# Four seven-product blocks per FFN, a third weight sum by transfer, x sums from PSUM, and a written list for splits and sums

## The chip, the cores and the metric

One core of a Trainium2 chip runs the kernel in one launch. The metric is device time in microseconds (us), the median of several executions.

## The reference

A trunk of two layers on `x` of 256 tokens and 1024 features, float32. Each layer is: a feed-forward network (FFN), a mixer (bidirectional mLSTM in layer 0, windowed attention in layer 1), and a second FFN, each with a residual and a layer norm. Cut to what matters:

```python
def swiglu(x, w_in, w_out):                 # w_in 1024 x 5632, w_out 2816 x 1024
    gu = x @ w_in
    g, u = gu[..., :D_FF], gu[..., D_FF:]
    return (jax.nn.silu(g) * u) @ w_out

for l in range(2):
    x = layer_norm(ALPHA * x + 0.5 * swiglu(x, ffn_w_in[l, 0], ffn_w_out[l, 0]), ...)
    y = mlstm_mixer(x, ...) if l == 0 else window_attention(x, ...)
    x = layer_norm(ALPHA * x + y, ...)
    x = layer_norm(ALPHA * x + 0.5 * swiglu(x, ffn_w_in[l, 1], ffn_w_out[l, 1]), ...)
```

So there are six stages: FFN, mLSTM, FFN, FFN, attention, FFN.

## The kernel before

*Precision.* Every operand of a large product is kept as two `fp32r` tiles: a high half (a cast on ACT, `w_hi`) and a low half (value minus high half, a subtraction on DVE, `w_lo`). A product takes three matmuls: high-high, high-low, low-high (`mm3`).

*Weights.* All weights of all stages go through one object, `Weights`. A *word* is 512 KB of weights, loaded into a raw tile by SP's queue (`w_raw`, 4 buffers, and `s_raw`, 6 buffers, for words that are added to each other; two more buffers `v_raw` in the FFNs). A *split* makes a high and a low half of a raw tile; `plan` is the fixed order of all splits, and PE uses them in that order. At most 10 splits are in the ring (`RING`): a new one needs the oldest to be used up. `high()` emits the cast, `low()` the subtraction, `sum()` the sum of two raw tiles; `sum()` is a DVE addition where both tiles are there, and where the second summand is a weight block in HBM it is an accumulating DMA issued from POOL's queue. `low()` frees the raw tile when it has no more uses, and `load()` issues the next loads.

*An FFN.* Eight `wide` words give the first 512 columns of `g` and `u`. Then follow three groups, each a *unit* and a *seven-product block*. A unit is 256 columns of `g` and of `u`, four words (`beside`), 48 matmuls of 512 columns. A seven-product block gives 512 columns of each. It regards the tokens as two halves and the features as two halves and multiplies the 2 x 2 blocks in seven products instead of eight, 84 matmuls: four products use sums of blocks of x (`S1` to `S4`) and sums of weight blocks. With `b11`, `b12` the first feature half of `g` and `u` and `b22` the second half of `u`, `b11` is split four times: as loaded, after adding `b12`, after adding `b22`, and after adding the second half of `g` from HBM (by transfer). `b12` is split once, after a sum with `b22` on DVE. That makes 14 splits, six DVE sums (`s_raw<-s_raw`) and two accumulating transfers a block. The x sums are taken from `xr`, two tiles that DVE adds from the high and low halves of the transposed x.

Behind a chunk of columns, the products with `w_out` follow as *down* rows: `down(n)` takes n splits and adds 12 matmuls each into the four `py` banks of PSUM. Six down rows are left for the end of the FFN, then come the norm and the transposes of the new x (`py` banks, `to_xT`). 22 down rows, 84 splits per FFN in all.

*Order of the work.* Each engine runs its instructions in the order in which the program emits them. Within FFNs a planner (`Paced`, with fixed costs per instruction) keeps an estimated time per engine and decides after each matmul whether a high half, a low half or a sum is emitted there (`fill`). In the other stages hand-written tables (`PU`, `TD`, `MP`, `PD`) say how many splits are emitted at which place.

In the profile almost all instructions carry L134, the line of the recording call of the planner; L263 is the accumulating transfer in `sum()`. Tiles are therefore told apart by name: `pw` and `py` are PSUM banks, `hh`, `e`, `g` the evacuated products, `h_hi`/`h_lo` their transposes.

Of the kernel before, what the change touches and what calls it, by code (L numbers as in the profile page):

```python
# [1 line left out]

# [15 lines left out]
S = 256  # L18
# [3 lines left out]
F = 2816  # L22
UNITS = F // 256
GROUPS = 3
# [4 lines left out]
PU = [3, 1, 2, 1, 1, 1, 1, 1, 0, 1, 1, 2]  # L29
# [4 lines left out]
TD = [0, 3, 2, 0, 2, 2]  # L34
MP = [1, 0, 0, 0, 1, 0, 1, 1, 0, 0, 0, 0, 2, 2, 2]
PD = [8, 0, 5, 9, 6]
# [3 lines left out]
AHEAD = 300.0  # L40
SOON = -1000.0
LANDING = 2200.0
LOADING = 1340.0
SECOND = 1250.0
ADDING = 8000.0


class Paced:

    def __init__(self, nc):
        self.nc = nc
        self.pe = self.vec = self.act = self.dma = 0.0
        self.there, self.places = {}, {}
        self.filler, self.alone = None, True
        self.vector = Engine(nc.vector, self.on_vector)
        self.scalar = Engine(nc.scalar, self.on_scalar)
        self.tensor = Engine(nc.tensor, self.on_tensor)
# [3 lines left out]

    def place(self, ap):

        f = ap.ap[0][0]
        key = (ap.offset % f if f else 0, tuple(ap.ap[1:]))
        if key not in self.places:
            i = np.array([key[0]])
            for step, n in key[1]:  # L70
                i = (i[:, None] + step * np.arange(n if step else 1)[None, :]).reshape(-1)
            self.places[key] = i
        return self.places[key]

    def when(self, *aps):
        t = 0.0
        for ap in aps:
            a = self.there.get(ap.name)
            if a is not None:
                i = self.place(ap)  # L80
                t = max(t, a[i[i < a.size]].max(initial=0.0))
        return t

    def mark(self, ap, t):
        i = self.place(ap)
        a = self.there.get(ap.name)
        if a is None or a.size <= i.max():
            self.there[ap.name] = np.zeros(int(i.max()) + 1)
            if a is not None:
                self.there[ap.name][:a.size] = a  # L90
        self.there[ap.name][i] = t

    def load(self, ap, source, engine=None):
        if engine is not None:
            engine.dma_start(ap, source)
        elif isinstance(source, list):
            for k, src in enumerate(source):
                self.nc.sync.dma_start(ap[:, k].rearrange("p (m f) -> p m f", m=src.shape[1]), src)
        else:
            self.nc.sync.dma_start(ap, source)  # L100
        come = self.pe + LANDING
        alone, self.alone = self.alone, come > self.dma
        self.dma = max(self.dma, come) + LOADING + (SECOND if alone and not self.alone else 0.0)
        self.mark(ap, self.dma)

    def on_vector(self, name, n, out, ins):
        self.vec = max(self.vec, self.when(*ins)) + (n + 71) / 0.96
        for o in out:
            self.mark(o, self.vec + 115)

    def on_scalar(self, name, n, out, ins):
        self.act = max(self.act, self.when(*ins)) + n * 0.912 + 25
        for o in out:
            self.mark(o, self.act + 125)

    def on_tensor(self, name, n, out, ins):
        self.pe = max(self.pe, self.when(*ins)) + (109.0 if name == "transpose" else n / 2.4 + 13.3)
        for o in out:
            self.mark(o, self.pe + 200)
        if self.filler is not None:  # L120
            self.filler()


class Engine:
    def __init__(self, engine, told):
        self.engine, self.told = engine, told

    def __getattr__(self, name):
        f = getattr(self.engine, name)
        if name.startswith("preload"):  # L130
            return f

        def call(out, *args, **kw):
            r = f(out, *args, **kw)  # L134
            ins = [x for x in [*args, *kw.values()] if hasattr(x, "ap")]
            outs = [out] + ([kw["accum_out"]] if "accum_out" in kw else [])
            size = lambda x: int(np.prod(x.shape[1:]))
            self.told(name, size(out) if name in ("matmul", "transpose") else max(map(size, [out] + ins)), outs, ins)
            return r
        return call  # L140


class Weights:
# [5 lines left out]
    def __init__(self, nc, pool, words, plan, after):  # L149
        self.nc, self.pool, self.words, self.plan, self.after = nc, pool, words, plan, after  # L150
        self.raw, self.parts, self.half, self.sums = {}, {}, [], []
# [4 lines left out]
        self.uses = [0] * len(words)  # L156
        for p in plan:
            self.uses[p["word"]] += 1
# [45 lines left out]
    def split(self, upto):  # L204
        while self.made < min(upto, len(self.plan)):
            self.high()
        while self.half and self.half[0][0] < upto:
            self.low()

    def high(self):  # L210

        nc, i = self.nc, self.made
        p = self.plan[i]
        while self.half and (p["word"] not in self.raw or any(h[0] == p["needs"] for h in self.half)):
            self.low()
        while any(s_[0] == p["needs"] or p["word"] not in self.raw for s_ in self.sums):
            self.sum()
        if p["word"] not in self.raw:
            return False
# [12 lines left out]
        return True  # L232

    def low(self):

        nc = self.nc
# [13 lines left out]
        self.sums += [(i, *sum_) for sum_ in self.after.get(i, ())]  # L250
# [3 lines left out]
    def sum(self):  # L254
        nc = self.nc
        _, w, v = self.sums.pop(0)
# [5 lines left out]
        else:  # L262
            nc.gpsimd.dma_start(t.rearrange("p (k f) -> p k f", k=self.words[w]["k"]), v, accum_op=OP.add)  # L263
            nc.mark(t, max(nc.vec, nc.pe) + ADDING)

    def fill(self):

        nc = self.nc
        while True:
            act, vec = max(nc.act, nc.pe), max(nc.vec, nc.pe)  # L270
            if act < nc.pe + AHEAD and len(self.half) < 2 and self.made < min(self.room, len(self.plan)):
                p = self.plan[self.made]
                if (p["word"] in self.raw and nc.when(self.raw[p["word"]]) < act + SOON
                        and not any(p["needs"] == x for x in [h[0] for h in self.half] + [s_[0] for s_ in self.sums])):
                    self.high()
                    continue
            if vec < nc.pe + AHEAD:
                if self.half and nc.when(self.half[0][1]) < vec + SOON:
                    self.low()
                    continue  # L280
                if self.sums and nc.when(*(self.raw[w] for w in self.sums[0][1:] if isinstance(w, int))) < vec + SOON:
                    self.sum()
                    continue
            break

    def take(self, n):
        i = self.used
        self.used += n
        self.split(self.used)
        return [self.parts[j] for j in range(i, i + n)]  # L290
# [4 lines left out]
    def done(self, upto=None, most=None, high_only=False):  # L295

# [5 lines left out]
        if self.nc.filler is not None:  # L302
            self.fill()
            return
        end = min(self.room if most is None else min(self.room, self.made + most), len(self.plan))
        while self.made < end and self.high():
            pass
        if not high_only:
            self.lows()

    def lows(self):
        while self.half:
            self.low()
# [3 lines left out]
def trunk_kernel(ctx: ExitStack, tc: tile.TileContext, x, ffn_w_in, ffn_w_out, ln_g, ln_b, ml_w_in, ml_gate_b,  # L317
                 ml_norm_g, ml_w_out, at_w_in, at_sink, at_w_out, out):
    nc = Paced(tc.nc)
# [40 lines left out]
    def seven(w, c0, c1, downs):  # L360

        at = lambda r0, c: [two(w, r0 + 256 * j, c) for j in range(2)]
        b12, b11, b22 = ([word(x, 2, "s_raw") for x in at(*p)] for p in ((0, c1), (0, c0), (512, c1)))
# [3 lines left out]
        for j in range(2):  # L367
            after[s1[j]] = [(b11[j], b12[j])]
        downs(0)
# [15 lines left out]
    for j, (kind, l, i, _) in enumerate(stages):  # L385
        if kind == "ffn":
# [10 lines left out]
            for g in range(GROUPS):  # L397
                c0 = 512 + 768 * g
                for a in range(4):
                    beside(wi, a * 256, c0, F + c0)  # L400
                down(2)
                seven(wi, c0 + 256, F + c0 + 256, lambda i_: down(1) if g < GROUPS - 1 or i_ < 2 else None)
            down(6)
# [32 lines left out]
    W = Weights(nc, wpool, words, plan, after)  # L436
    load_x(0, 0)
# [61 lines left out]
    def to_xT(t, src, bank, halves=range(2)):  # L499
        for h in halves:  # L500
# [3 lines left out]
            split_evac(pair(xT, A, slice(4 * h, 4 * h + 4), tok(t)), p)  # L504

    def warm(n):

        p = ybank((128, 4, 128))
# [12 lines left out]
    class Norm:  # L521
# [9 lines left out]
        def finish(self, spare):  # L531
# [10 lines left out]
            if len(cuts) == 1:  # L542
                W.done(0, spare)
# [5 lines left out]
            if len(cuts) > 1:  # L549
                W.done(0, spare)  # L550

    def tail(y, h, todo, first, norm, last, turn_at, between=None):

        for t in range(2):
            for o in range(2):
                final = t == 1 and o == 1
                for n, (c, (i, w)) in enumerate(todo[t]):
# [6 lines left out]
                    if final and n >= turn_at - 1:  # L564
                        W.done(i + 1, (0, 3, 0)[min(n - turn_at + 1, 2)])
                norm[t].half(o, y[t][o])
            norm[t].finish(t)
        W.done(most=TD[bound[0]])
# [6 lines left out]
    def ffn(l, i, n, pending, last):  # L575
        with ExitStack() as ph:
# [11 lines left out]
            if start:  # L588
                warm(10)
                to_xT(0, xt[0], ybank, (0,))  # L590
                W.split(1)
# [770 lines left out]
```

## Time and profile before

| what | value |
|---|---|
| time, median of 3 runs (lowest, highest) | 942.11 us (941.06, 942.29) |
| span of the profiled execution | 941.2 us |
| busy: PE, DVE, ACT, POOL | 98%, 85%, 58%, 11% |
| matmuls on PE | 4416 |
| moved by DMA | 187.54 MB, mean 199 GB/s |
| last matmul to the end of the span | 7.5 us |

The profiled execution has no time of its own beside its span; the median of the timed runs stands 0.9 us above the span. Busy shares are averages over the six stages; the FFNs run about from 0 to 188, 306 to 481, 481 to 660 and 761 to 941 us. A line of a group gives the count, busy time and mean duration in ns, then the engine's idle time just ahead and what ended it. Durations overlap a little where an engine is pipelined, so the time from start to start is shorter than the duration.

### The profile page before, as it was taken

The numbers are of one execution on the slowest core, as the hardware profiler recorded it, in microseconds if no ns is written. First come the engines' busy times: TensorE is split into PE (matmuls) and PEld (weight loads), VectorE is DVE, ScalarE is ACT, GpSimd is POOL, SyncE is SP. The second block draws the span as 40 slices with busy tenths as digits, with TensorE's granted clock in tenths as the row PEclk, the third lists the DMA queues.
The fourth block names the chain that finished last, engine by engine and source line by source line (L and its number), as shares of the span: only waits on it lengthen the run. The fifth ranks groups of instructions, "written<-read, shape, count | busy, mean of one in ns | idle before, by whom it ended". The sixth has DMA issues, their size and how long they took to land.

```text
span 941.2 us, 12338 instructions
## 1 busy us (share of the span) xinstructions
PE 925.3 (98%) x4416; PEld 766.4 (81%) x4416; DVE 800.0 (85%) x943; ACT 546.5 (58%) x781; POOL 103.2 (11%) x162
## 2 busy tenths in 40 slices
PE   9999999999999999999999999999999999999996
PEld 7788888889878787888888888887887788888885
DVE  6899997787697889988888899977878888898975
ACT  5656756347563548565535566563678554757460
POOL 0030101011111000101010101010544300000100
PEclk9999999999999999999999999999999999999999
DMA  7969773646534949685549597746543266769531
GB/s 267 358 154 338 209 265 75 216 134 204 177 108 145 314 150 327 173 327 134 180 155 338 132 324 210 249 90 200 175 147 104 68 215 254 229 219 306 162 91 45
DMA packets 98461, 187.54 MB, mean 199 GB/s; under 512 B 6720, under 2 KB 37456, under 8 KB 98400
## 3 DMA queue, kind: packets, MB, share of 16 engines
q1 hardware_dynamic: 91072, 173.04, 53.1%
q0 software_dynamic: 6752, 12.66, 8.4%
q10 hardware_dynamic: 576, 1.05, 0.3%
q8 instruction: 35, 0.57, 0.2%
q14 instruction: 26, 0.21, 0.1%
HBM read 185.68 MB, written 1.05 MB: 198 GB/s over the span
## 4 chain that ended last, share of the span: by engine, by line
PE 73%; DVE 12%; DMA 6%; ACT 4%; issue 3%; POOL 1%; SPq 0%; DVEq 0%; ACTq 0%
PE pw L134 46%; PE py L134 27%; DVE w_lo L134 5%; DMA w_raw<-in_ffn_w_in_dram 3%; ACT w_hi L134 2%; DMA w_raw<-in_ffn_w_out_dram 1%; DVE s_raw L134 1%; DMA s_raw<-in_ffn_w_in_dram 1%; ACT sc L134 1%; DVE h L134 1%; DVE o L134 1%; DVE e L134 1%; DMA w_raw<-in_ml_w_in_dram 0%; DVE pr_lo L134 0%; ACT xT_hi L134 0%
## 5 line engine op out<-in xcount | busy, mean ns | idle before, releaser
L134 DVE TENSOR_TENSOR w_lo<-w_raw,w_hi 128x1024 fp32r<-128x1024 f32 (+1 forms) x237 | 280.9, 1216 | 16.0 <-ACT w_hi L134 14.0
L134 ACT CAST w_hi<-w_raw 128x1024 fp32r<-128x1024 f32 (+1 forms) x237 | 240.4, 1049 | 75.4 <-DMA w_raw<-in_ffn_w_out_dram 21.7
L134 PE MATMUL pw<-w_hi,xT_hi 128*128 128x512 f32 x560 | 222.6, 397 | 0.2 <-ACT xT_hi L134 0.2
L134 PE MATMUL pw<-w_hi,xT_lo 128*128 128x512 f32 x560 | 218.9, 391 | 0.2 <-DVE xT_lo L134 0.2
L134 PE MATMUL pw<-w_lo,xT_hi 128*128 128x512 f32 x560 | 218.3, 390 | 0.2 <-DVE w_lo L134 0.2
L134 ACT CAST w_hi<-s_raw 128x1024 fp32r<-128x1024 f32 x144 | 148.4, 1052 | 94.1 <-DVE s_raw L134 58.3
L134 DVE TENSOR_TENSOR w_lo<-s_raw,w_hi 128x1024 fp32r<-128x1024 f32 x144 | 172.6, 1219 | 19.2 <-ACT w_hi L134 19.1
L134 PE MATMUL py<-w_hi,h_hi 128*128 128x512 f32 x352 | 138.2, 393 | 0.3 <-ACT h_hi L134 0.3
L134 PE MATMUL py<-w_hi,h_lo 128*128 128x512 f32 x352 | 137.4, 390 | 0.2 <-DVE h_lo L134 0.2
L134 PE MATMUL py<-w_lo,h_hi 128*128 128x512 f32 x352 | 137.1, 390 | 0.2 <-DVE w_lo L134 0.2
L134 PEld LDWEIGHTS pw<-w_hi,xT_lo 128*128 128x128 f32 x560 | 105.1, 188 | 23.7 <-DVE xT_lo L134 1.0
L134 PEld LDWEIGHTS pw<-w_lo,xT_hi 128*128 128x128 f32 x560 | 105.4, 188 | 21.3 <-DVE w_lo L134 0.9
L134 PEld LDWEIGHTS pw<-w_hi,xT_hi 128*128 128x128 f32 x560 | 105.3, 188 | 21.0 <-ACT xT_hi L134 1.0
L134 DVE TENSOR_TENSOR s_raw<-s_raw 128x1024 f32<-128x1024 f32 x72 | 87.0, 1219 | 0.6
L263 POOL DMA_DIRECT2D s_raw<-in_ffn_w_in_dram x24 | 29.2, 1215 | 496.9 <-DVE w_lo L134 378.7
L134 PEld LDWEIGHTS py<-w_hi,h_lo 128*128 128x128 f32 x352 | 66.1, 188 | 15.2 <-DVE h_lo L134 1.4
L134 PEld LDWEIGHTS py<-w_lo,h_hi 128*128 128x128 f32 x352 | 66.1, 188 | 13.9 <-DVE w_lo L134 0.6
L134 PEld LDWEIGHTS py<-w_hi,h_hi 128*128 128x128 f32 x352 | 66.1, 188 | 13.9 <-ACT h_hi L134 0.7
L134 PE MATMUL pw<-w_hi,S_hi 128*128 128x512 f32 x192 | 74.7, 389 | 0.0
L134 PE MATMUL pw<-w_hi,S_lo 128*128 128x512 f32 x192 | 74.7, 389 | 0.0
L134 PE MATMUL pw<-w_lo,S_hi 128*128 128x512 f32 x192 | 74.7, 389 | 0.0
L134 DVE TENSOR_TENSOR h_lo<-pw,h_hi 128x512 fp32r<-128x512 f32 x44 | 30.1, 687 | 24.5 <-ACT h_hi L134 24.4
(218 smaller groups left out, 1118.1 us busy)
## 6 DMA issues: line engine op xcount, KB each, us to landing
w_raw<-in_ffn_w_out_dram SPq DMA_DIRECT2D x88, 512.0 KB, 5.3
s_raw<-in_ffn_w_in_dram SPq DMA_DIRECT2D x72, 512.0 KB, 6.1
w_raw<-in_ffn_w_in_dram SPq DMA_DIRECT2D x56, 512.0 KB, 5.2
w_raw<-in_ffn_w_in_dram SPq DMA_DIRECT2D x96, 256.0 KB, 4.7
s_raw<-in_ffn_w_in_dram POOLq DMA_DIRECT2D x24, 512.0 KB, 6.1
w_raw<-in_ml_w_in_dram SPq DMA_DIRECT2D x24, 512.0 KB, 4.6
w_raw<-in_at_w_in_dram SPq DMA_DIRECT2D x12, 512.0 KB, 3.8
w_raw<-in_ml_w_out_dram SPq DMA_DIRECT2D x8, 512.0 KB, 3.8
```

The source lines that it names most:

```text
L134: r = f(out, *args, **kw)
L263: nc.gpsimd.dma_start(t.rearrange("p (k f) -> p k f", k=self.words[w]["k"]), v, accum_op=OP.add)
```

## The change

- The FFN's parts become: first chunk, block, block, unit, block, block, six down rows (`PARTS`). Four seven-product blocks and one unit instead of three of each; down rows follow the first two blocks one after each of four steps, two follow the unit, and the last block has two.
- Within a block `b12` gets its third summand from HBM, the second half of `u`, by an accumulating transfer right after its use as a summand, instead of a DVE sum with `b22` after the third split of `b11`. Four DVE sums and four accumulating transfers a block instead of six and two.
- The x sums no longer go through `xr`. They read the PSUM banks in which the transposes of x lie (`xp`); one bank is copied to SBUF by ACT (`a21`), since an operation reads one of its two inputs there.
- The planner and the tables are gone. A string, `ORDER`, lists all high halves (H), low halves (L), sums on DVE (S) and sums by transfer (A) of the whole kernel, each with the number of engine operations that are emitted since the previous entry. After every operation of any stage, entries that are due are emitted if what they need is there. What PE needs at once is emitted in any case.
- The warm-up transposes use a `pw` bank.

```diff
-GROUPS = 3
+PARTS = [("s", (1, 1, 1, 1)), ("s", (1, 1, 1, 1)), ("u", 2), ("s", (1, 1, 1, 1)), ("s", (1, 1, 0, 0))]
+TAIL = 6
+BY_DMA = (0, 1)
...
+ORDER = (
+    "H19L0H16L0H33L3H2L4H3H7L2H2L1L5H38H9L0L1S6H2L4H2L0S0H3H3H5L3L3H5L1L12S3S0A8A5H8L3A4H2L2A2H0H2L1H2H0H0H0H0L4L12"
...
 class Engine:
...
-            self.told(name, size(out) if name in ("matmul", "transpose") else max(map(size, [out] + ins)), outs, ins)
+            c.n += 1
+            if c.then is not None:
+                c.then()
...
+    def ready(self, what):
+        if what == "L":
+            return bool(self.half)
+        if what in self.sums:
+            q = self.sums[what]
+            return bool(q) and all(w in self.raw for w in q[0][1:] if isinstance(w, int)) and not any(
+                x[0] == q[0][0] for x in (self.sums["S"] if what == "A" else ()))
+        p = self.plan[self.made] if self.made < min(self.room, len(self.plan)) else None
+        return p is not None and p["word"] in self.raw and not any(
+            x[0] == p["needs"] and (len(x) == 2 or x[1] == p["word"])
+            for x in self.half + self.sums["S"] + self.sums["A"])
+
+    def run(self, upto=0):
+
+        while True:
+            early = self.made < upto or self.half and self.half[0][0] < upto
+            next_ = [(o[0], what) for what, o in self.order.items()
+                     if o and (early or o[0][0] <= self.nc.n) and self.ready(what)]
+            if not next_:
+                assert not early, (self.made, self.used, self.nc.n)
+                break
+            _, what = min(next_)
+            self.order[what].pop(0)
+            self.high() if what == "H" else self.low() if what == "L" else self.sum(what)
...
     def seven(w, c0, c1, downs):
 
         at = lambda r0, c: [two(w, r0 + 256 * j, c) for j in range(2)]
-        b12, b11, b22 = ([word(x, 2, "s_raw") for x in at(*p)] for p in ((0, c1), (0, c0), (512, c1)))
+        b11, b12, b22 = ([word(x, 2, "s_raw") for x in at(*p)] for p in ((0, c0), (0, c1), (512, c1)))
         s1 = [split_of(w_) for w_ in b11]
         for a in at(512, c0):
             piece(a, 2)
-        for j in range(2):
+        t3 = [None, None]
+        for j, a in enumerate(at(512, c1)):
             after[s1[j]] = [(b11[j], b12[j])]
+            if j in BY_DMA:
+                after[s1[j]].append((b12[j], a))
+                t3[j] = s1[j]
         downs(0)
         s5 = [split_of(w_, None, p) for w_, p in zip(b11, s1)]
         for j in range(2):
             after[s5[j]] = [(b11[j], b22[j])]
         s6 = [split_of(w_, None, p) for w_, p in zip(b11, s5)]
         for j, a in enumerate(at(512, c0)):
-            after[s6[j]] = [(b11[j], a), (b12[j], b22[j])]
+            after[s6[j]] = [(b11[j], a)]
+            if j not in BY_DMA:
+                after[s6[j]].append((b12[j], b22[j]))
+                t3[j] = s6[j]
         downs(1)
-        [split_of(w_, None, p) for w_, p in zip(b12, s6)]
+        [split_of(w_, None, p) for w_, p in zip(b12, t3)]
         for w_ in b22:
             split_of(w_)
         downs(2)
         [split_of(w_, None, p) for w_, p in zip(b11, s6)]
         downs(3)
...
             split_evac(pair(xT, A, slice(4 * h, 4 * h + 4), tok(t)), p)
+            xp[t, h] = p
...
-            def x_raw(t):
-                nc.vector.tensor_add(xr[t], xT[0][:, :, tok(t)].bitcast(F32), xT[1][:, :, tok(t)].bitcast(F32))
...
+            def x_copy():
+                f1["a21"] = temp("a21").rearrange("p (k m) -> p k m", k=4)
+                nc.scalar.copy(f1["a21"], xp[1, 0])
 
             def x_one():
-                f1["S1"] = x_sum("S1", xr[1][:, low], OP.subtract, xr[1][:, high])
+                f1["S1"] = x_sum("S1", f1["a21"], OP.subtract, xp[1, 1])
 
             def x_two():
-                f1["S2"] = x_sum("S2", f1["S1"], OP.subtract, xr[0][:, low])
+                f1["S2"] = x_sum("S2", f1["S1"], OP.subtract, xp[0, 0])
...
-            for g in range(GROUPS):
+            turns = [lambda t=t: tr(hB0, t, hs[t]) for t in range(0 if start else 1, 2)]
+            for g, (what, n_) in enumerate(PARTS):
+                if what == "u":
+                    turns = [unit(turns)]
+                    down(n_)
+                else:
+                    turns = [seven(n_, turns)]
```

More of the change, by code (lines that the diff above doesn't have):

```diff
@@ L263, in sum @@
             nc.gpsimd.dma_start(t.rearrange("p (k f) -> p k f", k=self.words[w]["k"]), v, accum_op=OP.add)
[L264 to L284, printed above, removed]
     def take(self, n):
@@ L301, in done @@
         self.room = max(self.room, upto + RING)
[L302 to L313, printed above, removed]
+        self.run()
 @with_exitstack
@@ L436, in trunk_kernel @@
     W = Weights(nc, wpool, words, plan, after)
+    W.room = RING
+    nc.then = W.run
     load_x(0, 0)
```

260 lines of the change are left out of this document (91 added, 169 removed).

## The prediction

> **What bounds the kernel now.** I read the page first, for the busy shares, and then the chain of work that ended last.
>
> ```profile
> span 941.2 us, 12338 instructions
> PE 925.3 (98%) x4416; PEld 766.4 (81%) x4416; DVE 800.0 (85%) x943; ACT 546.5 (58%) x781; POOL 103.2 (11%) x162
> PE 73%; DVE 12%; DMA 6%; ACT 4%; issue 3%; POOL 1%; SPq 0%; DVEq 0%; ACTq 0%
> ```
>
> PE is busy 98% of the span, yet only 73% of the chain is PE's. So there are places where PE has just been fed in time and the chain runs through whoever fed it. The chain in order of time shows both kinds. First a stretch in which PE alone sets the pace, then the start of the second feed-forward network (FFN):
>
> ```profile
> 66.65 5.44 PE pw L134 x24
> 80.71 11.37 PE pw L134 x52
> ...
> 320.74 11.74 DMA w_raw<-in_ffn_w_out_dram
> ...
> 351.48 2.27 DVE w_lo L134 x2
> 353.75 2.28 DVE s_raw L134 x2
> ...
> 363.19 2.27 DVE w_lo L134 x2
> ...
> 366.93 3.38 PE pw L134 x16
> ```
>
> 24 matmuls of 512 columns in 5.44 us are 0.2267 us each; the 52 are 48 of those and 4 transposes, so a transpose takes (11.37 - 48 x 0.2267)/4 = 0.12 us. From 313 to 367 us the chain leaves PE and goes through loads and then DVE. The stretches of time show how little room there is:
>
> ```profile
> core 0: us, PE busy (x) PEld busy (x) DVE busy (x) ACT busy (x) POOL busy (x), PEclk, DMA share, GB/s
> 306.00:366.00 60.00, 59.82 (x272) 48.68 (x270) 52.25 (x55) 36.21 (x45) 2.67 (x3) 1.00 0.75 241
> 366.00:481.00 115.00, 114.13 (x522) 94.09 (x521) 101.30 (x106) 66.20 (x80) 6.27 (x5) 1.00 0.66 211
> 660.50:761.00 100.50, 97.57 (x507) 79.25 (x505) 83.51 (x135) 68.54 (x164) 42.20 (x92) 1.00 0.37 119
> 80.71:128.41 47.70, 47.70 (x218) 39.47 (x217) 44.76 (x46) 32.27 (x38) 2.49 (x2) 1.00 0.83 283
> ```
>
> The first two rows are the second FFN: 175.0 us, PE 173.95 busy, DVE 153.6. The third row is the attention stage, where PE shows 2.9 us idle. The last is one whole group of the first FFN (unit, seven-product block, six down rows): PE never idle, DVE busy 44.76 of 47.70. PE bounds the kernel; DVE is right behind it in the FFNs. The granted clock is 1.00 everywhere that matters.
>
> **The change, part by part.** Counts are from the diff and from the order in which the changed kernel's instructions stand on each engine.
>
> *PE.* A seven-product block does with 84 matmuls what two units do with 96. There are four instead of three per FFN, so 12 fewer in each of four FFNs: 48 x 0.2267 = 10.9 us off the engine that is never idle. The number of transposes stays.
>
> *DVE.* The durations as they follow each other:
>
> ```profile
> 337.02 2.35 DVE L134 TENSOR_TENSOR s_raw<-s_raw 128x1024 f32<-128x1024 f32 x2
> 339.29 0.74 DVE L134 TENSOR_TENSOR hh<-sg,pw 128x256 f32<-128x256 f32 x2
> 339.95 1.22 DVE L134 TENSOR_TENSOR w_lo<-s_raw,w_hi 128x1024 fp32r<-128x1024 f32 x1
> ...
> 349.06 0.69 DVE L134 TENSOR_TENSOR h_lo<-pw,h_hi 128x512 fp32r<-128x512 f32 x1 [0.28 <-ACT h_hi L134]
> 349.67 1.22 DVE L134 TENSOR_TENSOR w_lo<-s_raw,w_hi 128x1024 fp32r<-128x1024 f32 x1
> L134 DVE TENSOR_TENSOR xr<-xT_hi,xT_lo x8: 1217/1218/1222, 17.1 to 775.2; 128x1024 f32<-128x1024 f32 x8
> L134 DVE TENSOR_TENSOR S_lo<-S,S_hi 128x512 fp32r<-128x512 f32 x16 | 11.1, 692 | 15.5 <-ACT S_hi L134 15.5
> ```
>
> Two weight sums take from 337.02 to 339.29, 1.135 us each; a 512-column operation 349.67 - 349.06 = 0.61; a 256-column one (339.95 - 339.29)/2 = 0.33. A split's low half and an `xr` addition have the size of a sum, so 1.135 too. Per FFN: 6 splits more (+6.8: four blocks of 14 and a unit of 4 against three of each), 2 weight sums fewer (16 against 18, -2.3), both `xr` additions gone (-2.3), one more block's evacuation (5 + 2 operations of 512, +4.3), two units' fewer (2 x (2 x 0.33 + 0.61), -2.5). Net +4.0 us, 15.9 over four FFNs: 816 of some 930 us, 88%. In the second FFN 157.6 against 175.0 - 2.7 = 172.3 us of PE, 91%. That still fits, but only on average.
>
> *The tight stretch.* Before, a unit with its down rows stood between any two seven-product blocks; now the blocks stand in pairs, and the first comes straight after the first chunk. A block with four down rows holds 84 + 48 = 132 matmuls and 8 transposes: 29.9 + 1.0 = 30.9 us of PE. DVE has 18 splits (20.4), 4 sums (4.5) and 7 operations of 0.61 (4.3): 29.2 us, 94%, for 62 us in a row. The last group row above shows 94% on DVE over 47.7 us with PE never idle, so it can be done, if DVE hardly waits. Where DVE waited before, the list acts: the `S_lo` operations stood idle 15.5 us for `S_hi`, about 3.9 per FFN just ahead of the tight place. In the changed order of the later FFNs a low half of a weight stands between each `S` and its `S_lo`, so I count that wait as gone there; in the first FFN two of the four still follow directly.
>
> *Transfers.* The plain loads keep their bytes (66 words per FFN); 10 accumulating transfers per FFN are added, 40 in all, 21 MB.
>
> ```profile
> q1 hardware_dynamic: 91072, 173.04, 53.1%
> q0 software_dynamic: 6752, 12.66, 8.4%
> 112.00:128.00 16.00, 16.00 (x74) 13.23 (x73) 14.73 (x16) 12.24 (x15) 0.00 (x0) 1.00 1.03 390
> s_raw<-in_ffn_w_in_dram POOLq DMA_DIRECT2D x24, 512.0 KB, 6.1
> L263 POOL DMA_DIRECT2D s_raw<-in_ffn_w_in_dram x24 | 29.2, 1215 | 496.9 <-DVE w_lo L134 378.7 <-DVE e L134 45.4 <-DVE S L134 36.6
> ```
>
> At full load plain words move at 390 GB/s: 0.524 MB in 1.34 us. Queue 0 is nearly only the 24 accumulations: 8.4% of 941.2 us over 24 is 3.3 us of all 16 engines each. A block with four down rows now asks for 12 x 1.34 + 4 x 3.3 = 29.3 us of transfer in 30.9 us, 95%; a whole FFN 66 x 1.34 + 16 x 3.3 = 141 of 172, 82%. That is the second thin margin, and no row of before shows accumulations beside a full load queue. Their issue costs POOL 40 x 1.2 = 49 us on an engine 11% busy: nothing, except in the first FFN, where the accumulations of the second block's `b11` stand behind the small loads on POOL's queue.
>
> *The chain within a block.*
>
> ```profile
> L134 ACT CAST w_hi<-s_raw 128x1024 fp32r<-128x1024 f32 x144 | 148.4, 1052 | 94.1 <-DVE s_raw L134 58.3 <-PE pw L134 15.2 <-issue 13.6
> ```
>
> The last use of `b11` needs: low half of its second difference done, accumulation (6.1 us to landing, the row further up), high half on ACT (1.05), low half. In the changed order seven low halves stand on DVE in between: 7 x 1.135 = 7.9 us of cover against 7.15. Before, two more sums of 1.135 stood there. It holds with 0.8 us if the accumulation finds the engines as free as before.
>
> *ACT* gets 24 more casts of 1.05 and two or three more copies and activations per FFN, about 30 us on 546.5; hidden, at 62% busy. *The x sums* now read the transposes' PSUM banks, so the four `py` banks are held until the last sum; the first down row comes after it in program order and starts late only if DVE is late there. *The list* takes splits out of the norm and attention code. The stalls it could remove outside the FFNs are the 2.9 us of the attention row and little else; I take 2 off.
>
> *The sum.* 941.2 - 10.9 = 930.3. The start of each FFN was already set by DVE and loads (chain rows from 320.74 on). There the unit's PE time (72 matmuls, 16.3 us) no longer covers the first block, while DVE loses only 6 splits, 2 sums, 2 `xr`, the unit's three operations and the 3.9 us wait, 6.8 + 2.3 + 2.3 + 1.3 + 3.9 = 16.6. The two balance to 0.3 us, so each FFN start stays as tight as it was, and any late transfer shows on PE. I bound what is lost there at 0 and 3 us per FFN (the 11.74 us landing in the chain is some 6 us over the accumulation's 6.1, and half of that has no cover) and take 1.2: +5. With -2 for attention the span comes to 933, and the timed runs' median stands 942.1 - 941.2 = 0.9 above the span: **934 us**.
>
> **The rivals.**
>
> *The list feeds PE everywhere.* No new stall and the 2.9 us of attention gone with those at FFN starts: 941.2 - 10.9 - 4 + 0.9 = 927. For it: low halves stand between dependent operations wherever I looked. Against it: DVE at 94% and transfers at 95% at the same time.
>
> *Accumulations land late and the kernel becomes slower.* The place is the last use of `b11`, and that of `b12`, in the back-to-back blocks. Sharing the engines with four plain words (4 x 1.34) moves a landing from 6.1 to 11.4 us, 4.5 past the cover of 7.9 less the cast. Over a pair of blocks DVE then idles 9 us; the run-ahead absorbs about 4 in the first pair and all in the second, so PE loses 5 to 6 per FFN: 930.3 + 22 + 0.9 = 953. It decides from about 2.7 us lost per FFN, which gives the 10.9 back. Against it: in the row from 112 to 128 us the engines were full for 16 us and PE ran through. [...]
>
> *The gain is given back.* DVE waits a little in every block, 2 to 3 us per FFN: 930.3 + 10 + 0.9 = 941, no change. The DVE share of 94% speaks for it, the removed `S_lo` waits against.
>
> **How the numbers follow.** My forecast (929 to 938) gets 0.50, the list that feeds PE everywhere (below 929) 0.22, the gain given back (938 to 946) 0.14, late accumulations (above 946) 0.14. The range of 8 in 10 takes in the forecast, most of the better case and part of the third: 925 to 945. A difference of 0.2%, 1.9 us, is about what a measurement of this kernel can tell from no change (its three runs lie within 1.2 us). Below 940.2 lie the first two and a third of the third case, 0.77; within 0.2% 0.07; slower 0.16.
>
> **What would show it.** Right: `x512` matmul groups with 48 fewer instructions at the same pace; PE still at 98%; DVE near 816 us; the chain's DVE pieces again only at FFN starts. Late accumulations would show as ACT `w_hi` waiting for `s_raw` transfers, landings well above 6.1 us, and PE waiting for DVE `w_lo` in the second block of a pair. Given-back gain would show as a PE share of 96 to 97% without such landings. A time under 927 would say that the FFN starts had slack that I did not see.

## The result, and the profile after

| | before | after |
|---|---|---|
| time, median (lowest to highest) | 941.84 us (941.06 to 942.29) | 935.93 us (935.19 to 937.32) |
| ratio | 1 | 0.9942, 95% interval [0.9929, 0.9955] |
| span of the profiled execution | 941.2 us | 933.4 us |

The change makes the kernel 5.9 us faster. The profiled execution of after took 935.19 us, 1.8 us over its span, and the other executions of the two kernels whose span is known stand 1.7 or 1.8 us above theirs. By that, as an estimate, the profiled execution of before, of span 941.2, took some 942.9 us, a little more than its median: the spans differ by 7.8 us, the medians by 5.9.

First the page of after: span and busy shares, the queue of the accumulating transfers, the chain by engine, and their landing (issues, KB each, median us from issue to landing).

```profile
span 933.4 us, 12378 instructions
PE 914.4 (98%) x4368; PEld 756.3 (81%) x4368; DVE 812.3 (87%) x955; ACT 574.3 (62%) x813; POOL 147.0 (16%) x202
q0 software_dynamic: 17632, 33.64, 21.6%
PE 75%; DVE 12%; DMA 5%; ACT 4%; issue 2%; POOL 0%; SPq 0%; DVEq 0%; ACTq 0%
s_raw<-in_ffn_w_in_dram POOLq DMA_DIRECT2D x64, 512.0 KB, 7.5
```

The 48 matmuls are gone, PE is still at 98% and has 75% of the chain (73% before), and DVE has 12 us more to do. Now both spans are cut into their six stages, each stage beginning with PE's first transpose of its new x: FFN, mLSTM, FFN, FFN, attention, FFN. Columns are as in the prediction's stretches of time (stretch, its length, busy us with count of PE, PEld, DVE, ACT and POOL, granted clock, DMA share, GB/s). Before:

```profile
0.00:185.96 185.96, 183.56 (x830) 151.43 (x831) 158.89 (x167) 109.51 (x132) 15.24 (x22) 1.00 0.74 238
185.96:296.70 110.74, 109.18 (x648) 95.54 (x647) 86.25 (x144) 60.20 (x113) 14.73 (x23) 1.00 0.47 153
296.70:478.79 182.09, 181.04 (x824) 148.62 (x823) 160.39 (x168) 106.75 (x128) 10.22 (x8) 1.00 0.68 220
478.79:658.19 179.40, 179.11 (x817) 147.53 (x816) 158.13 (x166) 104.26 (x126) 10.14 (x8) 1.00 0.68 217
658.19:753.04 94.85, 91.92 (x482) 74.60 (x481) 78.10 (x126) 65.35 (x160) 42.20 (x92) 1.00 0.38 123
753.04:941.20 188.16, 180.54 (x823) 148.65 (x821) 158.23 (x172) 100.42 (x122) 10.62 (x9) 0.99 0.60 190
```

After:

```profile
0.00:186.09 186.09, 181.18 (x819) 148.49 (x819) 161.27 (x169) 117.72 (x142) 26.37 (x32) 1.00 0.90 263
186.09:295.45 109.36, 108.15 (x648) 95.56 (x647) 86.83 (x146) 59.38 (x112) 15.21 (x23) 1.00 0.49 159
295.45:474.44 178.99, 178.03 (x811) 146.37 (x810) 163.01 (x171) 113.89 (x137) 22.41 (x18) 1.00 0.85 250
474.44:653.19 178.75, 177.12 (x805) 145.16 (x804) 160.22 (x169) 111.13 (x134) 22.28 (x18) 1.00 0.84 244
653.19:746.65 93.46, 91.31 (x482) 74.64 (x481) 78.40 (x128) 66.11 (x160) 39.04 (x92) 1.00 0.41 132
746.65:933.40 186.75, 178.55 (x811) 146.05 (x809) 162.54 (x176) 106.03 (x129) 21.74 (x19) 0.99 0.76 221
```

Each FFN should be 12 x 0.2267 = 2.72 us shorter. The second is (182.09 - 178.99 = 3.10). The first is no shorter at all (+0.13), the third and fourth by 0.65 and 1.41. So the four FFNs give back (what each falls short of 2.72) 2.85, -0.38, 2.07 and 1.31, together 5.85 of the 10.9 us. In a second profile of the changed kernel, of span 932.2 us, they give back 3.16, -0.26, 0.55 and 1.06, so one stage in one profile is known to about 1.5 us. The mLSTM and attention stages became 1.38 and 1.39 shorter. In sum -10.9 + 5.85 - 2.77 = -7.8, the difference of the spans.

Where PE still waits in the FFNs is seen at the start of the second. DVE's timeline of after (start, us, instruction, and in brackets idle time ahead and who ended it) runs from the low half of the transposed first chunk, `h_lo`, to `hh`, the next thing that PE needs:

```profile
317.59 0.69 DVE L94 TENSOR_TENSOR h_lo<-pw,h_hi 128x512 fp32r<-128x512 f32 x1 [0.67 <-ACT h_hi L94]
318.20 0.68 DVE L94 TENSOR_TENSOR S<-S,py 128x512 f32<-128x512 f32 x1
318.79 1.22 DVE L222 TENSOR_TENSOR w_lo<-w_raw,w_hi 128x1024 fp32r<-128x1024 f32 x1
319.93 0.68 DVE L94 TENSOR_TENSOR S_lo<-S,S_hi 128x512 fp32r<-128x512 f32 x1
...
323.47 1.21 DVE L222 TENSOR_TENSOR w_lo<-w_raw,w_hi 128x1024 fp32r<-128x1024 f32 x1
324.60 0.68 DVE L94 TENSOR_TENSOR S_lo<-S,S_hi 128x512 fp32r<-128x512 f32 x1
325.20 0.68 DVE L94 TENSOR_TENSOR hh<-sg,pw 128x512 f32<-128x512 f32 x1
```

DVE never idles in these 8.3 us: the x sums, their low halves and, between each sum and its low half, one weight's low half stand ahead of `hh`, and DVE took them one after the other, started 0.59 to 1.14 us apart. PE has 4 transposes and 36 matmuls (these 8.16 us) meanwhile, started before `h_lo` did, and then waits 1 us. PE's list of waits for the whole of after (us in all, times, longest) begins with this kind of wait; the list of before has none for `hh`:

```profile
PE pw L94 <- DVE hh L94: 3.1, 4, 1.0
```

In the stretch behind it, two blocks back to back, PE does not pause:

```profile
326.41:385.50 59.09, 59.09 (x268) 48.41 (x267) 53.45 (x54) 39.30 (x47) 8.46 (x7) 1.00 0.92 259
```

The four waits for `hh` are one at the start of each FFN. The chain (start, us, what) shows one more place, in the last pair of blocks of the third FFN:

```profile
618.52 9.43 DMA s_raw<-in_ffn_w_in_dram
...
633.36 1.14 DVE w_lo L222
```

A transfer that landed after 9.4 us was late for one block, and PE stood idle for 1.05 of the 8 us from 632 to 640. In the second profile of the changed kernel this place has no wait, and its third FFN took 177.2 us instead of 178.75.

### The profile page after: what moved, and what is told of

It is laid out like the page before. It is cut to its first block, busy times and chain, and to the rows that moved or that the text cites. A ratio compares the mean times of both kernels' runs of the same rounds, so it can differ in the third digit from the quotient of the medians.

```text
span 933.4 us, 12378 instructions
## 1 busy us (share of the span) xinstructions
PE 914.4 (98%) x4368; PEld 756.3 (81%) x4368; DVE 812.3 (87%) x955; ACT 574.3 (62%) x813; POOL 147.0 (16%) x202
## 3 DMA queue, kind: packets, MB, share of 16 engines
q0 software_dynamic: 17632, 33.64, 21.6%
q10 hardware_dynamic: 576, 1.05, 0.3%
HBM read 206.65 MB, written 1.05 MB: 223 GB/s over the span
## 4 chain that ended last, share of the span: by engine, by line
PE 75%; DVE 12%; DMA 5%; ACT 4%; issue 2%; POOL 0%; SPq 0%; DVEq 0%; ACTq 0%
PE pw L94 48%; PE py L94 28%; DVE w_lo L222 5%; DMA s_raw<-in_ffn_w_in_dram 2%; ACT w_hi L204 2%; DVE s_raw L236 1%; DMA w_raw<-in_ffn_w_out_dram 1%; DVE e L94 1%; ACT sc L94 1%; DVE S L94 1%; DVE h_lo L94 1%; DVE rm L94 1%; DVE S_lo L94 0%; DVE o L94 0%; DVE h L94 0%
## 5 line engine op out<-in xcount | busy, mean ns | idle before, releaser
L204 ACT CAST w_hi<-s_raw 128x1024 fp32r<-128x1024 f32 x192 | 197.4, 1051 | 112.6 <-DVE s_raw L236 83.9
L222 DVE TENSOR_TENSOR w_lo<-w_raw,w_hi 128x1024 fp32r<-128x1024 f32 x211 | 253.1, 1219 | 11.0 <-ACT w_hi L204 10.3
L222 DVE TENSOR_TENSOR w_lo<-s_raw,w_hi 128x1024 fp32r<-128x1024 f32 x192 | 229.5, 1220 | 24.3 <-ACT w_hi L204 23.7
L204 ACT CAST w_hi<-w_raw 128x1024 fp32r<-128x1024 f32 x211 | 214.3, 1050 | 44.8 <-DMA w_raw<-in_ffn_w_out_dram 9.8
L94 PE MATMUL pw<-w_hi,xT_hi 128*128 128x512 f32 x480 | 191.4, 399 | 0.7 <-ACT w_hi L204 0.7
L94 PE MATMUL pw<-w_hi,xT_lo 128*128 128x512 f32 x480 | 187.6, 391 | 0.0
L94 PE MATMUL pw<-w_lo,xT_hi 128*128 128x512 f32 x480 | 187.2, 390 | 0.1
L240 POOL DMA_DIRECT2D s_raw<-in_ffn_w_in_dram x64 | 77.7, 1227 | 477.8 <-DVE s_raw L236 183.2
L94 PE MATMUL pw<-w_lo,S_hi 128*128 128x512 f32 x256 | 100.3, 392 | 1.1 <-DVE w_lo L222 1.1
L94 PEld LDWEIGHTS pw<-w_lo,S_hi 128*128 128x128 f32 x256 | 48.1, 188 | 12.8 <-DVE w_lo L222 3.0
```

What stands on the lines that cost most here:

```text
L94: r = f(*args, **kw)
L204: nc.scalar.copy(hi, raw)
L222: nc.vector.tensor_sub(lo, raw, hi.bitcast(F32))
```

## The experiments

Each ratio is to the kernel before on the same chip. The changed kernel run a second time beside some of them gave 0.9933 [0.992, 0.9947] (936.39 us), so two or three us in a median are the least that tell kernels apart here.

> The changed kernel unaltered, on the same chip as the three beside it. Both theories: 0.994 of the kernel before, 5 to 7 us less.

**What each part is worth, with the planner in place of the list.** The parts were put into the kernel before, whose planner places splits and sums. First all of them, then the four blocks alone. To the kernel before:

```diff
-GROUPS = 3
+PARTS = [("s", (1, 1, 1, 1)), ("s", (1, 1, 1, 1)), ("u", 2), ("s", (1, 1, 1, 1)), ("s", (1, 1, 0, 0))]
+TAIL = 6
```

and for the run with all parts besides

```diff
+BY_DMA = (0, 1)
...
-                f1["S1"] = x_sum("S1", xr[1][:, low], OP.subtract, xr[1][:, high])
+                f1["S1"] = x_sum("S1", f1["a21"], OP.subtract, xp[1, 1])
```

> The changed kernel with its blocks, its third sum by transfer and its x sums from PSUM, but placed by the planner and the tables of before instead of the written list. Theory (the 48 matmuls give 10.9 us, and the list keeps DVE from waiting at the FFN starts): the S_lo operations wait for S_hi again, some 3 to 4 us per FFN at the place that has no slack, so 943 to 952 us, PE waits for w_lo in every first block. Rival (the list is worth nothing, the blocks alone make the time): 934 to 938 us.

> The kernel before with four blocks and one unit per FFN and nothing else: planner, third sum on DVE, x sums over xr. Theory: a block with four down rows asks DVE for 18 splits, 6 sums and 7 small operations, 31.5 us in 30.9 of PE, and each FFN start for two xr additions more; DVE bounds the first pair of blocks in each FFN: 4 to 8 us slower than the same blocks with the third sum by transfer under the planner, 948 to 960 us. Rival (DVE's run-ahead absorbs it): within 2 us of the other planner version.

Measured: 1007.39 us, 1.0691 [1.0672, 1.0709], with all parts; 1021.81 us, 1.0848 [1.0828, 1.0867], with the blocks alone. Both theories failed by 50 us and more: under the planner as it was, the new parts are a loss. Whether the planner could be fitted to them, and what a list would be worth with the old parts, was not tried. Of the first of the two, the page's busy shares, PE's waits, a piece of ACT's timeline, and stretches around the start of the second FFN:

```profile
PE 940.8 (93%) x4368; PEld 763.0 (76%) x4368; DVE 819.0 (81%) x955; ACT 575.0 (57%) x813; POOL 151.4 (15%) x202
```

```profile
PE pw L136 <- DVE w_lo L136: 17.4, 22, 2.5
PE pw L136 <- ACT w_hi L136: 10.0, 2, 9.4
PE pw L136 <- DVE hh L136: 9.3, 2, 4.7
```

```profile
336.84 1.05 ACT L136 CAST w_hi<-s_raw 128x1024 fp32r<-128x1024 f32 x1 [7.63 <-DMA s_raw<-in_ffn_w_in_dram]
```

```profile
344.60:354.40 9.80, 0.68 (x4) 0.22 (x2) 6.88 (x10) 4.59 (x8) 0.00 (x0) 0.77 0.76 215
354.65:359.81 5.16, 5.16 (x15) 4.20 (x15) 4.04 (x4) 1.82 (x3) 1.20 (x1) 0.50 0.37 53
```

PE stands still for 9.4 us at this place. First ACT's cast waits 7.6 us for a plain load into `s_raw`: SP issues these loads from 329.86 us on, 14.2 us after the stage began, where in after they start 11.4 us after it. Then each `S_lo` on DVE waits 0.7 us for ACT's `S_hi`, with `hh` behind the last of them. (PE's row of 9.4 us names ACT's `w_hi`, which ended at 354.62; the transposes that waited read `hh`, which DVE ended at 354.51.) Behind the pause PE runs at a granted clock of 0.50 for 5 us. Over the whole run the same 4368 matmuls are busy 26.4 us longer than in after (940.8 against 914.4).

All of the loss lies in the FFNs, each 14 to 19 us longer than before. The mLSTM and attention stages of this run, with the new parts but with the tables of before, take what they took before (110.74 and 94.85 us):

```profile
204.93:315.66 110.73, 109.14 (x647) 95.51 (x646) 86.25 (x144) 60.21 (x113) 14.71 (x23) 1.00 0.48 153
710.84:805.92 95.08, 92.11 (x481) 74.59 (x480) 79.11 (x128) 65.58 (x160) 42.20 (x92) 1.00 0.39 122
```

So the 2.8 us that after gains in these two stages (109.36 and 93.46) come from the list.

**Is it the exact places of the list?** First, the x sums were made from `xr` again, in the changed kernel.

```diff
-                nc.scalar.copy(f1["a21"], xp[1, 0])
+                x_raw(1)
...
+                x_raw(0)
-                f1["S2"] = x_sum("S2", f1["S1"], OP.subtract, xp[0, 0])
+                f1["S2"] = x_sum("S2", f1["S1"], OP.subtract, xr[0][:, low])
```

> The changed kernel with the x sums over xr as before (two DVE additions of 128x1024 per FFN more, no copy a21, no PSUM reads), list and blocks as changed. Theory (DVE work at the FFN starts comes out on PE one for one): 2.3 us more at each of four starts, 5 to 9 us slower than the changed kernel, about as slow as the kernel before. Rival (the start has cover): within 2 us of the changed kernel.

Measured: 999.54 us, 1.0617 [1.059, 1.0645], a loss of 63 us instead of 5 to 9. But `x_raw(0)` is one operation more per FFN, and the list counts operations: all later entries came one early. Three runs took the two apart.

Two are the changed kernel with the count shifted in `x_two` (for entries one operation late, `nc.n -= 1`):

```diff
+                nc.n += 1
                 f1["S2"] = x_sum("S2", f1["S1"], OP.subtract, xp[0, 0])
```

The third is the run with `xr` and its added operation past the count (`nc.nc` is the uncounted object):

```diff
-                nc.vector.tensor_add(xr[t], xT[0][:, :, tok(t)].bitcast(F32), xT[1][:, :, tok(t)].bitcast(F32))
+                (nc if t else nc.nc).vector.tensor_add(xr[t], xT[0][:, :, tok(t)].bitcast(F32), xT[1][:, :, tok(t)].bitcast(F32))
```

> Nothing is computed differently from the changed kernel: same instructions, same order on PE. Only the count of operations by which the list's entries come due is raised by one more in each of the four FFNs, at the second x sum, so that every later entry is emitted one operation early (four operations early by the last FFN). This is the shift that the run with x sums over xr had beside its additions. Theory (the written list's exact places carry the time, and the shift cost that run most of its 63 us): 40 to 65 us slower than the changed kernel, 975 to 1000 us. Rival (the additions of xr and the waits they bring cost it): within 3 us of the changed kernel, 934 to 939 us.

> As the run with the entries one operation early, with the count lowered by one in each FFN, so that every later entry comes one operation late. Theory (exact places carry the time in both directions): 10 to 60 us slower than the changed kernel. Rival (only the early side hurts, since an early cast or low half stands on its engine ahead of a small operation that PE waits for, while a late one has the ring's lead of up to 10 splits to spare): within 4 us, 934 to 940 us.

> The changed kernel with the x sums over xr as before, and the one added operation left out of the count, so that the list's entries stand where the changed kernel has them. Theory (the shift cost the run with xr its 63 us): what is left is 4 more additions on DVE at each FFN start, two of 1.2 us less the copy on ACT, 1 to 2.3 us per FFN: 4 to 9 us slower than the changed kernel, 940 to 946 us. Rival (the additions cost it): 990 to 1000 us again.

Measured: one operation early 991.66 us, 1.0542 [1.0503, 1.0581]; one late 980.37 us, 1.0407 [1.0391, 1.0422]; `xr` with the count right 945.77 us, 1.0039 [1.0024, 1.0055]. A shift by one operation per FFN costs 56 and 44 us with every instruction and PE's order unchanged, and the rival that only the early side hurts fails. Of the 55 us by which the span of the early run is longer, PE stands idle for 41 and is busy for 15 (929.1 us against 914.4). The additions themselves cost 9 to 10 us, just over the expected 4 to 9. They stand ahead of `hh` on DVE as the x sums do, and PE's waits for it go from 3.1 to 8.9 us; the rest is PE's busy time, 918.8 us against 914.4, at a mean granted clock of 0.994 against 0.998, with 0.50 behind one of these waits (last section):

```profile
PE pw L94 <- DVE hh L94: 8.9, 4, 2.9
```

What a shift does, on ACT with the entries early:

```profile
658.38 0.59 ACT L94 COPY e<-pw 128x512 f32<-128x512 f32 x1 [1.91 <-PE pw L94]
658.86 2.00 ACT L204 CAST w_hi<-s_raw 128x1024 fp32r<-128x1024 f32 x2
664.29 1.04 ACT L204 CAST w_hi<-s_raw 128x1024 fp32r<-128x1024 f32 x1 [3.43 <-DMA s_raw<-in_ffn_w_in_dram]
665.24 1.04 ACT L204 CAST w_hi<-w_raw 128x1024 fp32r<-128x1024 f32 x1
666.19 0.58 ACT L94 COPY e<-pw 128x512 f32<-128x512 f32 x1
```

The cast of the accumulated weight now stands ahead of the second copy `e`, which empties a PSUM bank. ACT waits 3.43 us for the transfer, and the copy and PE behind it wait too. In the changed kernel the same cast stands behind that copy, which no longer waits for the transfer. This is the transfer of 618.52 us shown above, so what its late landing costs there is the 1.05 us further on:

```profile
624.72 0.59 ACT L94 COPY e<-pw 128x512 f32<-128x512 f32 x1 [1.19 <-PE pw L94]
625.20 1.05 ACT L204 CAST w_hi<-s_raw 128x1024 fp32r<-128x1024 f32 x1
628.03 1.05 ACT L204 CAST w_hi<-s_raw 128x1024 fp32r<-128x1024 f32 x1 [1.78 <-DMA s_raw<-in_ffn_w_in_dram]
```

With the entries early, PE's largest waits are those for such a copy `e`. In all 13 a cast stands right ahead of the copy, and in 8 of them ACT had waited for a transfer into `s_raw` there, 0.2 to 4.5 us; in most of the others the casts alone were in the way. With the entries late the largest are others, for low halves and for `hh`:

```profile
PE pw L94 <- ACT e L94: 21.0, 13, 3.1
```

```profile
PE pw L94 <- DVE w_lo L222: 10.0, 14, 1.3
PE pw L94 <- DVE hh L94: 9.8, 3, 4.4
```

**The third sum by transfer.** One run put it back on DVE (16 blocks, two sums of 1.135 us each), one left the transfer out.

The first (in `ORDER` the 32 A entries of `b12` become S entries at the places of the later sums):

```diff
-BY_DMA = (0, 1)
+BY_DMA = ()
```

The second (`third` holds all `b12`):

```diff
-        else:
+        elif w not in self.third:
             nc.gpsimd.dma_start(t.rearrange("p (k f) -> p k f", k=self.words[w]["k"]), v, accum_op=OP.add)
```

> The changed kernel with the third weight sum on DVE (b12 plus b22 after the third split, as before), the list's entries for the 32 transfers turned into entries for sums at the place of the fourth sum. Theory: 32 sums of 1.135 us more on DVE, 36 us in all; the first pair of blocks of each FFN has no room (31.5 us of DVE in 30.9 of PE), so about 4.5 us per FFN come out on PE, 12 to 22 us slower than the changed kernel. Rival (transfers cost as much as they save, by landing late): within 4 us.

> The changed kernel without the 32 accumulations into b12 (the third weight sum is left out, so its products lack that summand); all else stands. Theory (what the FFNs give back is DVE work at their starts, accumulations cost little): 1 to 3 us faster than the changed kernel, 933 to 935 us, and the waits of PE for hh and for w_lo in the first block stay. Rival (accumulations that land late, 9 to 10 us instead of 6, hold the blocks): 5 us or more faster, 931 us or less, with those waits gone.

Measured: on DVE 949.85 us, 1.0081 [1.0067, 1.0094], 13.5 us over the changed kernel beside it; left out 935.38 us, 0.9924 [0.9911, 0.9936], 0.8 and 1.7 us below the two runs of the changed kernel (by their ratios 0.9933 and 0.9942). The first lies in what was expected. In the second the rival's 5 us or more is excluded, and PE's waits for `hh` stay (3.0 us); the theory's 1 to 3 us can't be told from no change. So the transfers cost next to nothing, 0 to 2 us, and the same sums on DVE cost 13.5 with a list that was made for the transfers. With the sums on DVE, PE waits for low halves 16 times, all in the first two blocks of an FFN, as the theory had it (`py` products first, then `pw`):

```profile
PE py L76 <- DVE w_lo L204: 4.9, 8, 0.6
PE pw L76 <- DVE w_lo L204: 4.6, 8, 0.7
```

**The start of the FFNs.** Three runs tried to take away the waits there: the transposes of the first chunk half a product later in the later FFNs; no sums on DVE in the first block; no sums at all in the first block.

The later turn, in `product()`, where `mid` holds the transposes for the first block:

```diff
                 for j in range(2):
+                    for f in mid if j else ():
+                        f()
                     w, = W.take(1)
```

Without the DVE sums (and without any: `b11 + b12`, and the same condition at the accumulating transfer):

```diff
+        if c0 == 512:
+            bare.update(b11)
...
+            if w not in self.bare:
+                nc.vector.tensor_add(t, t, self.raw[v])
```

> The changed kernel; in the three later FFNs the four transposes of the first chunk's second token half stand half a product (6 matmuls, 1.36 us) later in PE's order. Theory (PE waits there 0.74 to 1.12 us for hh, three times): 2 to 2.6 us faster, 933.5 us. Rival (the down row right behind then waits for h_hi and h_lo of these transposes, or DVE is as late at the next place): no change or up to 2 us slower.

> The changed kernel without the four DVE weight sums of the first block of each FFN (16 of 64 sums are left out, so these products use unsummed weights; casts, low halves and transfers stay). Theory (DVE bounds the first pair of blocks): 4.5 us of DVE less at each FFN start give back most of what the FFNs lose on PE, 4 to 7 us faster than the changed kernel, and w_lo ends some us further ahead of its use there. Rival (loads and accumulations bound the starts): 0 to 2 us faster, the landings and the casts' waits for them stay.

> In the first seven-product block of each FFN all sums of weight blocks are left out: the four on DVE (4 x 1.135 us) and the four by transfer (4 x 3.3 us of all 16 DMA engines); what the blocks give is wrong thereby, the matmuls, casts, low halves and plain loads stay. Theory (behind DVE the FFN start is bound by transfers just as tightly, so that taking away the DVE sums alone gained 0 to 2.5 us): with both limits relieved the about 5.9 us that the FFNs lost go for the most part: 4 to 6 us faster than the changed kernel, 930 to 932.5 us, and PE's waits for hh and w_lo at the FFN starts fall below 1 us in all. Rival (DVE's in-order queue of low halves, which stay, holds it): no better than without the DVE sums, 933.5 to 935 us, with the waits left.

Measured: the later turn 936.17 us, 0.993 [0.9917, 0.9943]; without DVE sums 933.91 us, 0.9908 [0.9894, 0.9922]; without any sums 933.67 us, 0.9905 [0.9887, 0.9923]. The later turn is no change, and the theory that it would help failed: the three waits for `hh` in the later FFNs go (0.9 us is left, in the first FFN), the span stays (933.3 against 933.4 us), and a new wait for DVE's `e` comes in the fourth:

```profile
PE pw L94 <- DVE e L94: 1.1, 1, 1.1
```

The other two gain at most 2 to 3 us, less than the theory of each had, and for the last of them the rival was right. Its first two rows of waits:

```profile
PE pw L94 <- ACT w_hi L204: 1.5, 2, 1.2
PE pw L94 <- DVE hh L94: 1.5, 3, 1.0
```

The 1.2 us for `w_hi` are at the end of the third FFN, at the place of the late transfer. In the second FFN the wait for `hh` stays at 1.0 us: the x sums and low halves ahead of `hh` are the same. In the third and fourth it falls from 0.6 to between 0.2 and 0.3 us, in the first it goes. The first FFN becomes shorter, 184.10 us, 2.0 less than in after. Without the DVE sums alone it took 186.47 us, without the `b12` transfers alone 185.36, and a second profile of the changed kernel gave 186.40: that fits a start held by sums on DVE and transfers together, where one taken away leaves the other. With one profile each, this is an indication and no more.

## Why the prediction was right

Forecast 934 us (929 to 938), measured 935.9.

- *48 matmuls, -10.9 us:* right. The count fell from 4416 to 4368, PE's busy time by 10.9 us (925.3 to 914.4), and the second FFN, where nothing was lost on balance, became shorter by its 2.72 us and a little more.
- *FFN starts, +5:* right in size, 5.85 in one profile and 4.5 in the other, but in part by luck. The price of 1.2 us was a choice between 0 and 3, and the 3 set the 11.74 us landing of a plain load (of its kind the median is 5.3 us) against the 6.1 of an accumulation. The places are less even than 1.2 each: about half in the first FFN, and at least 1 us by one late transfer at the end of the third, not at a start. Late transfers at a start the runs indicate only for the first FFN, and in part. In the later ones what shows is the order on DVE, `hh` behind the x sums, 0.6 to 1.0 us late, close to the balance that I had put at 0.3 us. More DVE work ahead of `hh` does cost time there (the `xr` additions), but taking these waits away gained none (the later turn), so what the later FFNs lose is not shown to be their price.
- *-2 outside the FFNs:* measured -2.77, and the run with the planner shows that it is the list's. The reason was right only in part: half of it is in the mLSTM stage, where I had put nothing, and in the attention stage PE's idle time, of which I took 2 us, fell only from 2.93 to 2.15 us.
- *The step from span to time failed.* I added 0.9 us, the distance of one execution's span from the median of others. An execution's own time is 1.8 us above its own span. The forecast span of 933 was nearly exact (933.4). Of the 1.9 us by which the time was low, 0.9 are this step, 0.4 the span, and 0.7 that the profiled execution was faster than its median (935.19 against 935.93). The profile of before, by the estimate above, belonged to a slower execution than its median.
- *DVE:* 812.3 us instead of 816, and the idle time ahead of `S_lo` went, as the order had shown (15.5 us before):

```profile
L94 DVE TENSOR_TENSOR S_lo<-S,S_hi 128x512 fp32r<-128x512 f32 x16 | 11.0, 686 | 2.8 <-ACT S_hi L94 2.8
```

- *The tight stretch:* in two back-to-back blocks of the second FFN DVE was busy 53.45 of 59.09 us, 90% for the forecast 94%, the transfers 92% for 95%, and PE never idle. Over whole FFNs the DMA share is 0.90, 0.85, 0.84 and 0.76, for 0.82. The engine time of an accumulation held too: 21.6% of 933.4 us over 64 is 3.15 us, for 3.3.
- *Cover within a block:* the margin of 0.8 us was too thin for the landing, which went from 6.1 to 7.5 us in the median. ACT does wait more for transfers into `s_raw` (`w_hi` before, and after); of the 28.3 us after, 23.9 are for accumulations, of the 6.8 before the trace shows none:

```profile
ACT w_hi L134 <- DMA s_raw<-in_ffn_w_in_dram: 6.8, 6, 2.0
```

```profile
ACT w_hi L204 <- DMA s_raw<-in_ffn_w_in_dram: 28.3, 18, 3.3
```

  Little of these 28 us reaches PE, which waits 0.7 us for `w_hi` and 1.1 us for its `w_lo` in all of after: the list mostly puts such casts behind the small operations, and the early run shows what the other order costs. So the rival of late accumulations did not come about, and the run without the `b12` transfers gained next to nothing. Its premise, a landing at 11.4 us, was too high: the median is 7.5, the longest 10.8.
- *ACT, POOL:* +27.8 us and +43.8 us busy for the forecast 30 and 49, both hidden.
- *Both other rivals:* a list that feeds PE everywhere (927) fails at the FFN starts; the gain given back in every block (941) fails in the tight stretch.
- *What I undervalued:* I gave the list 2 us, for the stages outside the FFNs. In the same program with the planner the parts lose 65 us, and with the entries one operation per FFN off 44 to 56. My balance of DVE, transfers and cover by sums of busy time was right for the order that I had read; it says nothing of another order, in which the same work stalls PE.

## What to carry to other kernels

When PE, DVE and the DMA engines are all nearly busy (96 to 99, 87 to 91 and 76 to 90% in the FFNs of after), sum the work to see whether it can fit, and then read the emitted order to see whether it does: one wide cast that waits for a transfer, ahead of the small copy that empties a PSUM bank, cost up to 3 us at a time here. Put waiting work behind the operations that free or feed the bound engine. Where DVE is short, try an accumulating transfer in place of a sum: here that cost next to nothing, though the DMA engines were 76 to 90% busy in the FFNs. A list of positions counted in operations must be made anew after any edit that adds or takes one, and an experiment on such a kernel must keep the count, or it measures the shift.

## What the runs showed of the hardware

*Some pauses of PE cost twice here.* In the run with the planner and all parts PE paused for 9.4 us up to 354.65, and ran from there to 359.81 us at a granted clock of 0.50: 15 matmuls and transposes in 5.16 us, 0.34 us each. The clock was 1.00 from 345 to 349 us, 0.59 from 349 to 354, still in the pause, and 1.00 again from 361.4 to 370, with 40 in 8.60 us, 0.215 us each. In after no such stretch is found ahead of the last matmul, where the clock is 0.99 or more in each 2 us, and PE's longest single wait there is 1.5 us. The clock was at 0.50 behind a shorter pause too. In the run with `xr` and the count right, the clock is 1.00 behind a pause of 2.2 us and 0.50 behind one of 2.8:

```profile
329.12:332.40 3.28, 3.27 (x17) 2.77 (x18) 3.25 (x3) 1.53 (x2) 1.20 (x1) 1.00 0.70 259
508.71:512.00 3.29, 3.29 (x10) 2.81 (x11) 3.26 (x3) 1.80 (x3) 1.70 (x2) 0.50 0.64 81
```

Yet behind the pause of 3.0 us up to 666.82 in the run with the entries early it is 1.00 (24 instructions of PE there in 5.77 us), so in these runs the length of a pause alone does not decide it. Of the 26 us more of PE busy time in the run with the planner some 13 are of this kind, an estimate from PE's busy time and its granted clock in stretches of 0.5 us.

*Accumulating transfers beside full loads.* With 64 instead of 24 of them, and the DMA engines 84 to 90% busy in the first three FFNs, their landing went only from 6.1 to 7.5 us in the median.
